# Encoder trunk on one core: output and down projections in 1024-column groups, seven block products for eight in 32 tile pairs

## The chip, the core and the metric

The kernel runs on one core of one Trainium2 chip. A core has a matrix engine (TensorE, PE in the profile), a vector engine (VectorE, DVE), an engine for activations and copies (ScalarE, ACT), a general engine (GpSimd, POOL) and an engine that here only issues DMAs (SyncE, SP). Each runs its own queue in order; they wait for one another through semaphores. Operands lie in SBUF; matmuls write to eight PSUM banks of 128 x 512 float32. The metric is the device time of one execution in microseconds (us), the median of several runs.

## The reference, cut to what matters

```
def mixer_block(x, ...):
    h = rms_norm(x, g_norm)
    uv, qkv, gates = split(h @ w_in)                 # 2048 -> 2048 | 3072 | 4096
    y_a = gmlp_branch(uv, ...)                       # u * (W_s LN(v) + b), 128-position chunks
    y_b = neighbourhood_attn(q, k, v, rpb)           # 16 heads, 4 x 16 window
    merged = sigmoid(g_a) * (y_a @ Wb_a) + sigmoid(g_b) * (y_b @ Wb_b)
    return x + merged @ w_out                        # "out": 2048 x 2048

def conv_ffn(x, ...):
    h = rms_norm(x, g_norm)
    up = conv3(h @ w_up)                             # "up": 2048 x 11008, depthwise over positions
    gate, val = split(up)
    return x + (silu(gate) * val) @ w_down           # "down": 5504 x 2048

out = rms_norm(conv_ffn(mixer_block(x, ...), ...), norm_final)
```

There is one layer, 256 positions (two blocks of 128), width 2048, all in float32.

## The kernel before, in words

Every product of float32 matrices is made of three matmuls. An operand is split into a high half, its rounding to the matmul's input type, and a low half, the rest: x = xh + xl, w = wh + wl. The products xh wh, xl wh and xh wl are summed in PSUM.

The weights are packed on the host into pieces of up to 128 x 1024 float32 (512 KB), in the order of use. For each piece SP issues a load into `wraw` (five buffers), ACT writes the high half `whi` as a copy, and DVE writes the low half `wlo` as wraw - whi. `begin(i)`, called ahead of the matmuls of piece i, issues the loads up to piece i + 5 and the splits up to piece i + 3, and runs the small tasks that were set for piece i with `at(i, f)`. So the order of all engines' work is that of one written program, whose unit is the piece. Buffers are reused in rotation.

There are two kinds of groups. In "nat" groups the activations are the stationary operand: for 512 output columns and both position blocks, two banks collect all rows of the weight; a piece is two weight tiles of 128 x 512 and takes 12 matmuls of 128 x 512. In "ws" groups the weights are stationary and the activations stream; these are u, q, k and the up-projection. The up-projection has 22 groups of two channel tiles (gate and value; the last has one), eight pieces each. After each, ACT and DVE add the banks' two halves, multiply by the norm, do the convolution (`conv`, lines 754 to 761), the gate (766, 767), and split the activation `a` (362, 363). Only after all 22 do the four down groups of 512 columns run over the 43 activation tiles. At a group's end `ev_down` adds the banks to x2 (line 781), squares the sum for the norm (782) and multiplies by the final gain (791). The output projection is the same with 16 tiles of `m`, and `ev_out` adds x (`xr`). The last group ends with its last four pieces in order of the position block, and `finish` scales and stores each block.

## Time and profile before

| | |
|---|---|
| runs | 1331.11 us median of 3 (1330.84 to 1331.73) |
| profiled execution | 1331.94 us, of which the instructions span 1329.9 |
| granted TensorE clock | 0.997 |
| DMA | 261.40 MB, mean 197 GB/s |
| stages in the span, us | start and value, u: 0 to 125; attention, gates, branches: 125 to 575; output: about 575 to 617; up: 617 to 1086; down: 1086 to 1321 |

In the page, the first part gives busy time per engine, the second the span in 40 slices (digits are tenths). The chain of waits is followed back from the last instruction. In a list of groups the columns are line, engine, operation, output <- inputs, shapes, count, busy us, mean ns of one, and the idle time ahead of them with what ended it. In the timeline the columns are start, length, engine, line. Matmuls overlap, so that their mean length is longer than the time from one to the next.

### The profile page before, as it was taken

To read this page: it belongs to the slowest core of one execution; us is meant where nothing else is said; L and a number is where in the kernel's file an instruction comes from. 1 tells how busy PE (TensorE), PEld (TensorE's weight loads), DVE (VectorE), ACT (ScalarE), POOL (GpSimd) and SP (SyncE) were. 2 spreads that over 40 slices of the span, in tenths; PEclk is the share of its full clock that TensorE was granted. 3 is DMA by queue.
4 is the path that set the end of the run, shared out by engine and by line. 5 is a ranking of instruction groups with operands and counts; after the bars stand their busy time and mean duration, and the time that the engine had idled before them with its cause. 6 is when DMAs were issued, how large, how long until landed. Compare 5 with 4: busy or idle time off the path is not lost.

```text
span 1329.9 us, 18442 instructions
## 1 busy us (share of the span) xinstructions
PE 1317.1 (99%) x6817; PEld 1124.5 (85%) x6817; DVE 868.5 (65%) x1248; ACT 721.8 (54%) x1059; POOL 100.2 (8%) x192
## 2 busy tenths in 40 slices
PE   8999999999999999999999999999999999999997
PEld 6888888888888888888888888888888888888885
DVE  6576667777564545555878787878787875545454
ACT  6755567576444444545656565656565564434342
POOL 0501065430000000000000000000000000000000
PEclk9999999999999999999999999999999999999998
DMA  9856786655666667666666666666666567656662
GB/s 359 280 185 183 212 225 180 202 159 180 187 189 189 193 189 224 206 201 181 188 190 189 191 189 190 189 191 188 191 186 193 164 196 222 211 186 205 190 199 95
DMA packets 77082, 261.40 MB, mean 197 GB/s; under 512 B 9792, under 2 KB 13760, under 8 KB 76736
## 3 DMA queue, kind: packets, MB, share of 16 engines
q1 hardware_dynamic: 72592, 252.40, 61.5%
q0 software_dynamic: 3968, 7.30, 2.4%
q8 instruction: 53, 0.87, 0.3%
q10 hardware_dynamic: 432, 0.53, 0.1%
q14 instruction: 37, 0.30, 0.1%
HBM read 256.00 MB, written 2.10 MB: 194 GB/s over the span
## 4 chain that ended last, share of the span: by engine, by line
PE 98%; DMA 1%; DVE 0%; SPq 0%; ACT 0%; issue 0%; DVEq 0%
PE bank L235 30%; PE bank L256 17%; PE bank L258 17%; PE bank L257 17%; PE bank L239 16%; DMA wraw<-in_weights_dram 1%; PE bank L592 1%; PE bank L642 0%; PE bank L468 0%; PE bank L730 0%; PE bank L688 0%; PE bank L632 0%; SPq L300 0%; DVE x L820 0%; SPq L177 0%; DVE wlo L192 0%
## 5 line engine op out<-in xcount | busy, mean ns | idle before, releaser
L192 DVE TENSOR_TENSOR wlo<-wraw,whi 128x1024 fp32r<-128x1024 f32 (+1 forms) x473 | 571.4, 1212 | 385.1 <-ACT whi L191 371.5
L191 ACT ACTIVATE whi<-wraw 128x1024 fp32r<-128x1024 f32 (+1 forms) x473 | 492.5, 1045 | 395.4 <-PE bank L257 278.2
L235 PE MATMUL bank<-h,whi 128*128 128x512 f32 x1760 | 423.1, 391 | 0.0
L235 PEld LDWEIGHTS bank<-h,whi 128*128 128x128 f32 x1760 | 322.9, 188 | 61.7
L239 PEld LDWEIGHTS bank<-h,wlo 128*128 128x128 f32 x1760 | 226.4, 191 | 9.0
L239 PE MATMUL bank<-h,wlo 128*128 128x256 f32 x1760 | 230.8, 283 | 0.0
L256 PE MATMUL bank<-whi,h 128*128 128x512 f32 x384 | 151.7, 395 | 0.9 <-ACT h L352 0.6
L257 PE MATMUL bank<-whi,h 128*128 128x512 f32 x384 | 150.0, 391 | 0.8 <-DVE h L359 0.8
L258 PE MATMUL bank<-wlo,h 128*128 128x512 f32 x384 | 150.0, 391 | 0.6 <-DVE wlo L192 0.5
L256 PE MATMUL bank<-whi,a 128*128 128x512 f32 x344 | 133.9, 389 | 0.0
L257 PE MATMUL bank<-whi,a 128*128 128x512 f32 x344 | 133.9, 389 | 0.0
L258 PE MATMUL bank<-wlo,a 128*128 128x512 f32 x344 | 133.9, 389 | 0.0
L256 PEld LDWEIGHTS bank<-whi,h 128*128 128x128 f32 x384 | 72.3, 188 | 16.4 <-ACT h L352 1.0
L257 PEld LDWEIGHTS bank<-whi,h 128*128 128x128 f32 x384 | 72.2, 188 | 16.4 <-DVE h L359 2.0
L258 PEld LDWEIGHTS bank<-wlo,h 128*128 128x128 f32 x384 | 72.1, 188 | 16.4 <-DVE wlo L192 1.5
L756 ACT ACTIVATE tc<-ta,vec 128x256 f32<-128x256 f32 x86 | 47.1, 595 | 70.1 <-DVE ta L754 70.1
L257 PEld LDWEIGHTS bank<-whi,a 128*128 128x128 f32 x344 | 64.6, 188 | 13.5
L256 PEld LDWEIGHTS bank<-whi,a 128*128 128x128 f32 x344 | 64.6, 188 | 13.3
L258 PEld LDWEIGHTS bank<-wlo,a 128*128 128x128 f32 x344 | 64.6, 188 | 13.3
L746 ACT ACTIVATE tb<-bank 128x256 f32<-128x256 f32 x86 | 28.3, 384 | 43.0 <-PE bank L235 42.7
L759 DVE SCALAR_TENSOR_TENSOR tc<-ta,vec,tc 128x255 f32<-128x255 f32 x86 | 41.4, 481 | 14.4 <-ACT tc L756 14.4
L959 POOL DMA_DIRECT2D gfin<-in_norm_final_dram x4 | 2.2, 549 | 642.9 <-DVE tc L767 535.5
(141 smaller groups left out, 1093.6 us busy)
## 6 DMA issues: line engine op xcount, KB each, us to landing
wraw<-in_weights_dram SPq DMA_DIRECT2D x459, 512.0 KB, 4.2
wraw<-in_weights_dram SPq DMA_DIRECT2D x14, 256.0 KB, 3.0
xs<-in_x_dram SPq DMA_DIRECT2D x2, 1024.0 KB, 9.0
vw<-va POOLq DMA_DIRECT2D x32, 64.0 KB, 6.2
xr<-in_x_dram POOLq DMA_DIRECT2D x4, 512.0 KB, 5.5
run<-in_rpb_dram POOLq DMA_DIRECT2D x64, 31.2 KB, 3.9
xk<-in_x_turned_dram SPq DMA_DIRECT2D x7, 256.0 KB, 7.8
gfin<-in_norm_final_dram POOLq DMA_DIRECT2D x4, 256.0 KB, 4.9
```

The source lines that it names most:

```text
L191: nc.scalar.activation(h[:, k, :m], w[:, k, :m], AF.Copy)
L192: nc.vector.tensor_sub(l[:, k, :m], w[:, k, :m], h[:, k, :m].bitcast(F32))
L235: nc.tensor.matmul(p, h[:, k - k0, b * 128:(b + 1) * 128], acts(k), start=k == 0, stop=k == nk - 1)
L239: nc.tensor.matmul(p[:, :T], l[:, k - k0, b * 128:(b + 1) * 128], acts(k)[:, 0, :], start=False, stop=False)
L256: nc.tensor.matmul(p, xh, h[:, kk, :m], start=st, stop=False)
L257: nc.tensor.matmul(p, xl, h[:, kk, :m], start=False, stop=False)
L258: nc.tensor.matmul(p, xh, l[:, kk, :m], start=False, stop=sp)
L592: nc.tensor.matmul(o, Q[s][:, c], k.rearrange("p (r c) -> p r c", r=ROWS)[:, :, k0:k0 + UNION], start=n == 0, stop=n == 1)
L746: nc.scalar.activation(t, p[:, T:], AF.Copy)
L756: nc.scalar.activation(v, u, AF.Identity, scale=ck[:, 1, ch:ch + 1], bias=ck[:, 3, ch:ch + 1])
L759: nc.vector.scalar_tensor_tensor(v[:, 1:], u[:, :T - 1], ck[:, 0, ch:ch + 1], v[:, 1:], op0=OP.mult, op1=OP.add)
L959: nc.gpsimd.dma_start(fin["g", j], bass.AP(tensor=norm_final.tensor, offset=norm_final.offset + j * 512, ap=[[0, 128], [1, 512]]))
```

## The change

**Groups of 1024 columns.** The value columns, the output and the down projection use "wide" groups: a piece is one weight tile of 128 x 1024, and four banks (two position blocks by two column halves) collect the sums. An ordinary piece takes 12 matmuls as before.

**Seven products.** A pair of tiles (256 rows of the weight) by two position blocks and two column halves is a 2 x 2 by 2 x 2 block product, eight block products of three matmuls. In four of the pairs of each wide group of output and down (`OUT_SEVEN`, `FF_SEVEN`; 8 pairs in the output, 24 in down) it is made of seven, of sums of blocks. The sums of activation blocks are made by GpSimd (`token_sums`) and split once; the sums of weight blocks are made by DVE from the two raw tiles, in place, for every pair and column group (`sums`): a half unit `half_hi`, `half_lo` (512 columns) and three units of 1024 (b, t, s) instead of two. The seven products go to eight banks, four of which collect parts that `combine` joins after the last such pair; the joined block `comb` is added to x2, by DVE or by a DMA that adds.

**Low halves by DMA.** Of the ordinary pieces in these groups every second (25 in all) gets its low half in another way: ACT writes -w rounded to `wlo`, a DMA of GpSimd's queue adds w to it.

**Three channel blocks.** Up and down alternate: 7 up groups and their part of down, 7 and theirs, 8 and theirs; down's sums are added to x2 after each block (six wide groups instead of four). 

**Queues.** Pieces are prepared up to i + 4, as far as units (four, six from the output on) are free; a raw buffer is loaded again as soon as the program has split it. Banks are handed out in the order in which they were freed. x is loaded into x2 by two DMAs, the four loads of `xr` are gone. At the start one chunk of x goes with each piece, instead of two.

```diff
+AHEAD = 5
+RAW, UNITS, HALVES = (5, 0), (4, 2), 2
+FF_BLOCKS = ((0, 14), (14, 28), (28, 43))
+FF_SEVEN = (0, 1, 3, 5)
+FF_ORDER = (0, 1, 2, 3, 4, 5, 6)
+OUT_SEVEN = (4, 5, 6, 7)
+OUT_ORDER = ((0, 1, 4, 5, 2, 6, 7, 3), (4, 5, 0, 6, 1, 7, 2, 3))
+LAST = 3
...
+            if i in by_dma:
+                nc.scalar.activation(l[:, :size], w[:, :size], AF.Copy, scale=-1.0)
+                nc.gpsimd.dma_start(l[:, :size], w[:, :size], accum_op=OP.add)
+                high(h[:, :size], w[:, :size])
+                raw_done(i)
+                return
...
+        def one():
+            slot = half_free.pop(0)
+            h, l = (slot[0].tile([128, 512], F32R, name=f"half_{p}{slot[1]}") for p in ("hi", "lo"))
+            halves[i] = (h, l, slot)
+            r0 = raw[i][0]
+            high(h, r0[:, c0])
+            low(l, r0[:, c0], h)
+            nc.vector.tensor_add(r0[:, c0], r0[:, c0], r0[:, c1])
+        def two():
+            r0, r1 = raw[i][0], raw[i + 1][0]
+            hb, lb = unit((i, "b"))
+            ht, lt = unit((i, "t"))
+            high(hb, r1)
+            nc.vector.tensor_add(r0[:, c1], r0[:, c1], r1[:, c1])
+            high(ht, r0)
+            low(lb, r1, hb)
+            nc.vector.tensor_add(r1[:, c1], r1[:, c1], r0[:, c0])
+            nc.vector.tensor_add(r1[:, c0], r1[:, c0], r1[:, c1])
+            low(lt, r0, ht)
+            raw_done(i)
+        def three():
+            r1 = raw[i + 1][0]
+            h, l = unit((i, "s"))
+            high(h, r1)
+        def four():
+            r1 = raw[i + 1][0]
+            h, l, _ = units[i, "s"]
+            low(l, r1, h)
+            raw_done(i + 1)
...
+        def combine():
+            c = fx["p"].tile([128, 4, 512], F32, name="comb")
+            nc.scalar.activation(c[:, 0, :], p(1), AF.Copy)
+            nc.vector.tensor_sub(c[:, 1, :], c[:, 0, :], p(6))
+            nc.vector.tensor_sub(c[:, 2, :], c[:, 1, :], p(7))
+            nc.vector.tensor_sub(c[:, 3, :], p(5), c[:, 2, :])
+            nc.vector.tensor_sub(c[:, 1, :], p(5), c[:, 1, :])
+            free(p(1), p(6), p(7), p(5))
...
+            if n in firsts:
+                product(1, acts(k, 0), (h, l))
+                product(5, S[0], (ht[:, c0], lt[:, c0]))
+                product(7, S[2], (ht[:, c1], lt[:, c1]))
...
+            elif n - 1 in firsts:
+                product(6, S[1], (hs[:, c1], ls[:, c1]))
+                product(2, acts(k + 1, 0), (hb[:, c0], lb[:, c0]))
+                product(3, S[3], (hb[:, c1], lb[:, c1]))
+                product(4, acts(k + 1, 1), (hs[:, c0], ls[:, c0]))
...
+    def token_sums(f, a11, a21, a12, a22):
+        nc.gpsimd.tensor_sub(f[:, 4, :], f[:, a21, :], f[:, a11, :])
+        nc.gpsimd.tensor_sub(f[:, 5, :], f[:, a21, :], f[:, a22, :])
+        nc.gpsimd.tensor_sub(f[:, 6, :], f[:, a11, :], f[:, 5, :])
+        nc.gpsimd.tensor_sub(f[:, 7, :], f[:, a12, :], f[:, 6, :])
...
+    def rest_by_dma(j):
+        def go(c):
+            nc.gpsimd.dma_start(rs["x2"][:, :, j * 1024:(j + 1) * 1024], c.rearrange("p (b a) t -> p b (a t)", b=2),
+                                accum_op=OP.add)
...
+    for j in range(2):
+        steps["out", j] = wide_step(("out", j), of_tiles(lambda k: mg["mT"][k]), lambda k: four_sums(fx["s", k], 0),
+                                    ("before", (rest_by_dma, rest_by_sums)[j](j)), ev_out(j))
...
+            rest = ("before", rest_by_sums(j)) if end else ("after", rest_by_dma(j))
+            steps["down", n, j] = wide_step(("down", n, j), down_acts, down_sums, rest, ev_down(n, j),
+                                            LAST if end and j == 1 else 0)
```

How the queues stand at the places of which the prediction speaks (a row is line, operation, output <- inputs, columns, and in brackets the engines and DMA queues that it waits for):

VectorE in the down projection before, at the change from one group of 512 columns to the next: low halves, the two additions into x2, two multiplies by the final gain.

```order
L192 TENSOR_TENSOR wlo<-wraw,whi 128x1024 [waits DMAHW1_49,PE_49,Activation_49]
L192 TENSOR_TENSOR wlo<-wraw,whi 128x1024 [waits DMAHW2_49,PE_49,Activation_49]
L781 TENSOR_TENSOR x_4942<-bank,x_4942 128x512 [waits PE_49] x2
L791 TENSOR_TENSOR x_4942<-x_4942,gfin 128x512 [waits DMASW4_49,Activation_49]
L791 TENSOR_TENSOR x_4942<-x_4942,gfin 128x512 [waits Activation_49]
L192 TENSOR_TENSOR wlo<-wraw,whi 128x1024 [waits DMAHW3_49,Activation_49]
```

VectorE now, at the change of column group in the first channel block: "one" of the next group's second pair (L245 into `half_lo`, L289), the last low half of its first pair, "two" of the second pair (L296 to the L245 ahead of L969), then the additions into x2 that empty the four banks.

```order
L245 TENSOR_TENSOR half_lo_7644<-wraw_7572,half_hi_7643 128x512 [waits DMAHW1_49,Activation_49]
L289 TENSOR_TENSOR wraw_7572<-wraw_7572 128x512 [waits DVE_49]
L245 TENSOR_TENSOR wlo_7641<-wraw_7550,whi_7640 128x1024 [waits PE_49]
L296 TENSOR_TENSOR wraw_7572<-wraw_7572,wraw_7574 128x512 [waits DMAHW2_49,DVE_49]
L245 TENSOR_TENSOR wlo_7664<-wraw_7574,whi_7663 128x1024 [waits PE_49,Activation_49]
L299 TENSOR_TENSOR wraw_7574<-wraw_7574,wraw_7572 128x512 [waits DVE_49]
L300 TENSOR_TENSOR wraw_7574<-wraw_7574 128x512 [waits DVE_49]
L245 TENSOR_TENSOR wlo_7666<-wraw_7572,whi_7665 128x1024 [waits PE_49,Activation_49]
L969 TENSOR_TENSOR x_4941<-bank_7390,x_4941 128x512 [waits PE_49]
L969 TENSOR_TENSOR x_4941<-bank_7394,x_4941 128x512 [waits PE_49]
L969 TENSOR_TENSOR x_4941<-bank_7398,x_4941 128x512 [waits PE_49]
L969 TENSOR_TENSOR x_4941<-bank_7483,x_4941 128x512 [waits PE_49]
```

A pair's two low halves have become eight instructions, and the additions stand behind a whole pair's preparation.

PE before, in a down group: a piece waits for its high half and its low half.

```order
L256 MATMUL bank_10499<-whi_10753,a32_5613 128x512 [waits Activation_49]
L257 MATMUL bank_10499<-whi_10753,a32_5613 128x512
L258 MATMUL bank_10499<-wlo_10754,a32_5613 128x512 [waits DVE_49]
L256 MATMUL bank_10499<-whi_10753,a33_5614 128x512
L257 MATMUL bank_10499<-whi_10753,a33_5614 128x512
L258 MATMUL bank_10499<-wlo_10754,a33_5614 128x512
```

PE now, at the place of the VectorE rows: the second half of the next group's first pair, products 6, 2, 3 and 4; banks 7717, 7721 and 7725 are those that the additions into x2 empty.

```order
L384 MATMUL bank_7713<-whi_7640,a_6146 128x512 [waits DVE_49,Activation_49]
L385 MATMUL bank_7713<-whi_7640,a_6146 128x512
L386 MATMUL bank_7713<-wlo_7641,a_6146 128x512 [waits DVE_49]
L384 MATMUL bank_7717<-whi_7609,a_6146 128x512 [waits DVE_49]
L385 MATMUL bank_7717<-whi_7609,a_6146 128x512
L386 MATMUL bank_7717<-wlo_7610,a_6146 128x512
L384 MATMUL bank_7721<-whi_7609,a_6146 128x512 [waits DVE_49]
L385 MATMUL bank_7721<-whi_7609,a_6146 128x512
L386 MATMUL bank_7721<-wlo_7610,a_6146 128x512
L384 MATMUL bank_7725<-whi_7640,a_6146 128x512 [waits DVE_49]
```

Three products now wait for DVE's additions, where before a group found its banks free.

More of the change, by code (lines that the diff above doesn't have):

```diff
@@ L962, in trunk_kernel @@
     fin["load"] = load_fin
[L963 to L967 removed]
+    at(starts["down", end, 1], sqrt_ready)
+    for i, piece in enumerate(pieces):
+        key = piece[0]
+        if i == starts[key] and key in before:
+            before[key]()
+        begin(i)
+        steps[key](i)
     finish_tasks()
```

725 lines of the change are left out of this document (454 added, 271 removed).

## The prediction

> **What bounds the kernel now.** First the page: busy shares, the slices, the chain of waits.
>
> ```profile
> PE 1317.1 (99%) x6817; PEld 1124.5 (85%) x6817; DVE 868.5 (65%) x1248; ACT 721.8 (54%) x1059; POOL 100.2 (8%) x192
> PE   8999999999999999999999999999999999999997
> DVE  6576667777564545555878787878787875545454
> PE 98%; DMA 1%; DVE 0%; SPq 0%; ACT 0%; issue 0%; DVEq 0%
> ```
>
> TensorE (PE) is the bound everywhere: 98% of the chain, no gaps but at both ends. VectorE (DVE) is next, and unevenly: 7 and 8 tenths in the up-projection (slices 20 to 32), 4 and 5 in the down-projection. The windows of the up stage and of one down group give numbers, and the timeline gives the rate of PE.
>
> ```profile
> 617.00:1077.00 460.00, 460.00 (x2645) 406.64 (x2644) 352.40 (x574) 268.65 (x413) 0.00 (x0) 1.00 0.62 185
> 1145.00:1203.00 58.00, 58.00 (x257) 48.04 (x257) 28.92 (x26) 23.70 (x26) 0.54 (x1) 1.00 0.61 199
> ...
> 1086.80 0.39 PE L256 MATMUL bank<-whi,a 128*128 128x512 f32 x1
> 1320.50 0.39 PE L258 MATMUL bank<-wlo,a 128*128 128x512 f32 x1
> ...
> L256 PE MATMUL bank<-whi,a 128*128 128x512 f32 x344 | 133.9, 389 | 0.0
> ```
>
> The columns after the length are busy us of PE, weight load, DVE, ACT, POOL. DVE is busy 77% of the up stage and 50% of a down group. The mean of 389 ns is not what a matmul costs, since they overlap: L256, L257 and L258 have 344 each, so 1032 start between 1086.80 and 1320.50, one per 233.7/1031 = 0.2267 us. This is the price that I use.
>
> The price of DVE is also read from start to start.
>
> ```profile
> 790.41 0.76 DVE L754 TENSOR_TENSOR ta<-ta,rb 128x256 f32<-128x256 f32 x2
> 791.50 0.49 DVE L759 SCALAR_TENSOR_TENSOR tc<-ta,vec,tc 128x255 f32<-128x255 f32 x1 [0.33 <-ACT tc L756]
> 792.02 0.48 DVE L761 SCALAR_TENSOR_TENSOR tc<-ta,vec,tc 128x255 f32<-128x255 f32 x1
> 792.43 0.48 DVE L759 SCALAR_TENSOR_TENSOR tc<-ta,vec,tc 128x255 f32<-128x255 f32 x1
> 792.94 0.48 DVE L761 SCALAR_TENSOR_TENSOR tc<-ta,vec,tc 128x255 f32<-128x255 f32 x1
> 793.34 1.22 DVE L192 TENSOR_TENSOR wlo<-wraw,whi 128x1024 fp32r<-128x1024 f32 x1
> 794.48 0.42 DVE L767 TENSOR_TENSOR tc<-tc 128x256 f32<-128x256 f32 x1
> 794.84 1.23 DVE L192 TENSOR_TENSOR wlo<-wraw,whi 128x1024 fp32r<-128x1024 f32 x1
> ...
> 808.37 1.42 DVE L748 TENSOR_TENSOR ta<-bank,tb 128x256 f32<-128x256 f32 x4 [1.17 <-ACT tb L746]
> ...
> 1081.16 0.69 DVE L192 TENSOR_TENSOR wlo<-wraw,whi 128x512 fp32r<-128x512 f32 x1
> 1081.76 0.42 DVE L767 TENSOR_TENSOR tc<-tc 128x256 f32<-128x256 f32 x1
> ```
>
> A low half of 1024 columns takes 1.14 us (793.34 to 794.48), one of 512 takes 0.60, a multiply of 256 takes 0.36. An instruction that waits for the one ahead of it starts 0.52 after it, one that doesn't 0.41: such a wait costs 0.11. A convolution step takes 2.93 (790.41 to 793.34).
>
> **The change, part by part.** PE: 32 pairs do 21 matmuls for 24, so 96 fall away: 96 x 0.2267 = **-21.8 us**. A seven-product pair takes 4.76 us of PE, a plain pair 5.44; an up piece stays (22.3 us for a full group of eight, half for the last).
>
> DVE, for a seven-product pair: three lows of 1024, one of 512, four sums of 512 (no row of before; nearest the 512 low): 3 x 1.14 + 5 x 0.60 = 6.4, and four waits on the instruction ahead: **6.9 us**, where the two lows of before were 2.3. Of this "one" is 1.4, "two" 4.3, the last low 1.1. A plain pair costs 1.14, its second piece being made by DMA. The change of DVE per pair is +4.6 while PE's share falls: a pair needs 2.1 us more of DVE than PE takes for it. A column group has 4 x 6.9 + 3 x 1.14 + 2.7 (four instructions that join the sums) + 2.45 (four additions into x2) = 36.2 us of DVE against 4 x 4.76 + 3 x 5.44 = 35.4 of PE. So in a down block DVE has no slack, and it enters with a debt, the convolutions of the last two up groups, against a lead of four or five pieces.
>
> *Blocks one and two.* Zero is when PE starts the last up group; PE would need the last low of the second column group at 22.3 + 70.7 - 5.4 - 2.7 = 84.9. DVE has until then 8 x 6.9 + 6 x 1.14 + 4.6 (four up lows) + 10.3 and 8.7 (evacuating two up groups: four additions 1.4 and in the first 1.2 of waiting, two convolutions, gates, splits) + 2.7 + 2.45 = 90.8. **5.9 us** can't be hidden by any order. Followed in the order that stands (adding the prices row by row, and each instruction waiting for its own): the first pair is ready in time; the second's low at 31.2 where PE wants it at 29.6, having waited 0.5 already; the third pair's first half at 40.3 for 39.4, its last low at 45.6 for 42.4; the fourth in time. That is 0.5 + 1.7 + 0.9 + 3.2 = 6.3. Then the change of group: the first product that needs a new bank comes 2.7 us into the pair, at 66.7, but the addition that empties the bank stands behind "two" of the next pair but one on DVE and ends at 70.6: +3.9. After it the second group is ahead. **+10.2 each**, 20.4.
>
> *Block three.* The last up group has half the columns: 11.1 us of PE while DVE must still do the convolutions of the group ahead. First pair ready at 17.5 for 11.1 (+6.4), then +1.2, +1.6, +1.3, +0.8, +0.6. At the change of group DVE also adds the joined sums to x2 (2 x 1.14), and each addition is now followed by its multiply, which waits for a square on ACT:
>
> ```profile
> 1146.13 1.28 DVE L781 TENSOR_TENSOR x<-bank,x 128x512 f32<-128x512 f32 x2
> 1147.39 0.19 ACT L782 ACTIVATION_READ_ACCUMULATOR junk<-x 128x1 f32 x1
> 1147.61 1.45 DVE L791 TENSOR_TENSOR x<-x,gfin 128x512 f32<-128x512 f32 x2 [0.19 <-ACT junk L782]
> ```
>
> From the first addition to the first multiply are 1.48 us, so each bank follows the last by 2.05. The third bank is free at 74.6 where PE could use it at about 65: 9.4, and 3 more for the next pair's low behind it. **+24.2**. The sum of DVE alone: 8 x 6.9 + 7 x 1.14 + 12.2 (the full group ahead, with four half-size lows) + 4.3 (the last group) + 5.0 (joining, and into x2) + 8 x 0.6 (additions and multiplies) = 89.5 against 11.1 + 76.2 - 10.9 = 76.4 of PE, 13.1 at least.
>
> *Output projection.* DVE: 8 x 6.9 + 5 x 1.14 + 2.4 (the last branch) + 2.6 (m and its sums split) + 2.7 + 2.45 + 3.4 (splitting the transposed x2) = 74.5 for 70.9 of PE, 3.6 at least. At the change of group the joined sums go to x2 by a DMA of 1 MB with addition, and the additions, and the transposes that PE has ahead of its next product, wait for it.
>
> ```profile
> xs<-in_x_dram SPq DMA_DIRECT2D x2, 1024.0 KB, 9.0
> xr<-in_x_dram POOLq DMA_DIRECT2D x4, 512.0 KB, 5.5
> ```
>
> Joined at 43.3, landed at 43.3 + 1 (issue) + 9.0 (the same size, without addition), three additions: 55.2, where PE stands at 45.0. With 2 us later for the transposes and the squares on ACT: **+12.3**, between 3.6 and 21 (twice the landing). The Trainium skill, "DMA: Bandwidth & Descriptors", section "Anatomy of one DMA", gives 2 us and bytes at 436 GB/s for this queue, by which 1 MB would be an estimated 4.4 us; the trace has 9.0 beside weight loads, and by the page's figure this term would be 7.7.
>
> *The 25 low halves made by DMA.*
>
> ```profile
> L191 ACT ACTIVATE whi<-wraw 128x1024 fp32r<-128x1024 f32 x459 | 483.9, 1058 | 383.5 <-PE bank L257 271.5 <-PE bank L235 92.7 <-DMA wraw<-in_weights_dram 7.5
> ```
>
> ACT gets a second copy of 1.06 for each; with 3.8 for a seven-product pair it does 4 x 3.8 + 9 x 1.06 = 25 us in a group of 35, so it stays clear. The 512 KB need 5.5 to, reading two sources, 9 us; the plain piece after two seven-product pairs has its buffer 7.5 us ahead and ACT's copy first, so 0 to 3 us late, in 8 places. Lateness there gives DVE time it lacks next: I take 0, and 20 as the other end.
>
> *The end.* The last two blocks of the output finish 2.05 us apart instead of 4.8 (nine matmuls for 21):
>
> ```profile
> 1320.92 0.69 DVE L781 TENSOR_TENSOR x<-bank,x 128x512 f32<-128x512 f32 x1 [0.43 <-PE bank L258]
> 1324.71 0.54 DVE L820 TENSOR_SCALAR x<-h,r,e 128x512 f32<-128x512 f32 x1
> ```
>
> One finish occupies DVE 4.3 us, so the second starts 2.4 to 3 us later: **+2.9**.
>
> *The start.* One x chunk per piece instead of two: 640 KB for 768.
>
> ```profile
> 0.00:45.00 45.00, 41.25 (x173) 32.61 (x174) 26.04 (x34) 30.27 (x51) 0.71 (x6) 1.00 0.96 371
> ```
>
> PE idles 3.75 us there, and the data that it waits for falls by a sixth: -0.7, between -2 and +1. The value columns in one group: same matmuls, 0. x goes to x2 directly, two DMAs on POOL's queue for four; twelve activation pairs split 896 columns for 512, 0.4 us on ACT and DVE in the up stage's slack: 0.
>
> *GpSimd's sums* (four of 128x128 for 16 pairs) lie under up pieces. What they do to DVE shows where POOL masks the bias:
>
> ```profile
> 194.56 0.50 POOL L557 TENSOR_SCALAR_AFFINE_SELECT bias<-bias 64x256 f32<-64x256 f32 x1
> 203.95 1.32 DVE L192 TENSOR_TENSOR wlo<-wraw,whi 128x1024 fp32r<-128x1024 f32 x1
> 204.28 1.36 POOL L557 TENSOR_SCALAR_AFFINE_SELECT bias<-bias 64x256 f32<-64x256 f32 x1
> ```
>
> The same select takes 1.36 for 0.50 beside a low, and the low 1.32 for 1.22: 0.1 per low, four lows a pair, hidden by DVE's 23% but for the last pairs before each block, 0.4 there: 0. The Trainium skill, "SBUF — State Buffer", section "Who interferes with whom", states that a VectorE instruction with two SBUF inputs and a GpSimd instruction that reads SBUF exclude each other for a whole instruction. The trace agrees on POOL's side; by the rule DVE could lose up to four POOL instructions of 0.5 us in each of the three last groups, an estimated 6 us more.
>
> Sum: -21.8 + 20.4 + 24.2 + 12.3 + 2.9 - 0.7 = **+37.3**. The profiled execution took 1331.94 (span 1329.9), 0.8 over the median of 1331.11; +37.3 on the median is 1368.4.
>
> **Rivals.**
> *A: only DVE's sum counts, order costs nothing.* 2 x 5.9 + 13.1 + 3.6 = 28.5 instead of 56.9: 1340. For it: six units of buffer, and a PE that waits lets DVE get ahead. Against: additions behind "two" in a queue that runs in order.
> *B: faster.* It needs cheaper pairs. Per 0.1 us on a pair the four stages change by 8 x 0.1 each, 3.2 in all; with order's costs as they are the balance is at 5.7 us a pair, under A at 6.6. For it: my sums of 512 have no row; at 0.35 us (what four of 256 from PSUM take each, 1.42/4) the four cost 1.0 less, 5.9, and with A's order no stall is left, 1331.1 - 21.8 + 2.2 = 1311.5; with half of that cheapness 1324. Against: the 512 low has the same two SBUF inputs and takes 0.60.
> *C: the DMA sums bind.* If 512 KB with addition lands in 12 us, the eight early places lose 3 or more and the 1 MB lands 9 later: +20 and +9, 1388 to 1397. Against: the xr row.
>
> **How the numbers follow.** The order as followed 0.62, A 0.16, B 0.12, C 0.10. Two per mille (2.7 us) is what can be told from no change. The forecast is 1368, its own range 1352 to 1383; with A and C 1334 to 1393, which leaves out B and the far end of C. Faster 0.12, same 0.03 (the edge between A and B), slower 0.85.
>
> **What would show it.** Right: in the down blocks of the changed kernel DVE busy at nine tenths and more, PE at eight to nine; PE waiting for low halves from DVE; at each change of column group one wait of 4 us (blocks one, two), about 9 (block three) and about 10 (output) for additions to x2; seven-product pair at 6.9 us of DVE. B is right if the sums of 512 start 0.4 us apart; C if PE's waits name the DMA queue of the low halves. The forecast is wrong if DVE shows idle time in the down blocks while PE runs without gaps.

## The result, and the profile after

The changed kernel takes 1425.58 us (median of four, 1424.38 to 1426.46) against 1331.28 for the kernel before: ratio 1.0708, interval 1.0689 to 1.0726. It is slower, as forecast, but by 94 us, not 37; the time lies outside the range that was given (1334 to 1393).

First the page of the changed kernel: busy shares, the slices of PE, DVE and the granted clock, the chain, the two costliest groups that wait, and the transfers that are new.

```profile
PE 1337.3 (94%) x6721; PEld 1125.6 (79%) x6721; DVE 1024.6 (72%) x1450; ACT 790.1 (55%) x1141; POOL 187.4 (13%) x284
PE   9999999999999998699999888999988899998875
DVE  5586667766645569677878886687889668788777
PEclk9999999999999999799999899999998999999978
PE 72%; DVE 9%; issue 7%; DMA 6%; ACT 5%; SPq 0%; POOL 0%; DVEq 0%; ACTq 0%; POOLq 0%
...
L386 PE MATMUL bank<-wlo,a 128*128 128x512 f32 x296 | 126.0, 426 | 26.9 <-DMA wlo<-wraw 14.9
L384 PE MATMUL bank<-whi,a 128*128 128x512 f32 x296 | 125.8, 425 | 22.8 <-DVE x L969 12.6
...
wlo<-wraw POOLq DMA_DIRECT2D x25, 512.0 KB, 7.7
x<-comb POOLq DMA_DIRECT2D x5, 1024.0 KB, 12.1
```

PE's share of the chain falls from 98% to 72%, and the gaps stand in four places only: slices 16 and 17 (output) and the three down blocks. PE is busy 20 us longer than before though it has 96 matmuls fewer; the mean of a down matmul rises from 389 ns to between 418 and 426, and PEclk shows 7 and 8 where it had shown 9. VectorE (DVE) is at 8 and 9 tenths in the first two slices of blocks one and two, but at 6 in the third (slices 25 and 32), where PE has gaps as well: DVE's work alone doesn't explain them.

The timeline of PE in block one shows what a wait looks like and what follows it (the number in brackets is the idle time ahead, and what ended it).

```profile
788.25 0.39 PE L384 MATMUL bank<-half_hi,a 128*128 128x512 f32 x1
...
790.74 0.39 PE L386 MATMUL bank<-wlo,a 128*128 128x512 f32 x1
794.54 0.80 PE L384 MATMUL bank<-whi,a 128*128 128x512 f32 x1 [3.41 <-DVE ta L685]
795.13 0.63 PE L385 MATMUL bank<-whi,a 128*128 128x512 f32 x1
795.55 0.63 PE L386 MATMUL bank<-wlo,a 128*128 128x512 f32 x1
...
800.67 0.45 PE L386 MATMUL bank<-wlo,a 128*128 128x512 f32 x1
800.96 0.39 PE L384 MATMUL bank<-whi,a 128*128 128x512 f32 x1
...
815.05 0.79 PE L386 MATMUL bank<-wlo,a 128*128 128x512 f32 x1 [2.58 <-DVE wlo L245]
...
841.99 0.80 PE L384 MATMUL bank<-whi,a 128*128 128x512 f32 x1 [3.12 <-DVE x L969]
...
858.49 0.56 PE L386 MATMUL bank<-wlo,a 128*128 128x512 f32 x1 [4.77 <-DMA wlo<-wraw]
...
883.78 1.98 PE L369 MATMUL bank<-h,whi 128*128 128x512 f32 x8
```

There are four kinds of wait: for a bank that DVE empties after the last up group (L685), for a low half made by DVE, for a bank of the group ahead (the additions, L969), and for a low half made by DMA. After the longer ones matmuls start 0.427 us apart (795.13 to 795.55), for 0.227: thirteen of them here, 133 in the whole program, each some 0.2 us later than at full pace. My first reading was: 133 x 0.2 = 26.6 us for the clock, the rest for idling.

A stage is measured from the start of its first product to that of the next stage (block one: 788.25 to 883.78, 95.5), block three to the end of its last product. TensorE's own work in it is 70.8 in blocks one and two, 76.4 in block three and 84.3 in the output: the lengths of the kernel without pairs (e1 below) less 8 x 0.68. In us:

| kernel | output | block 1 | block 2 | block 3 | whole |
|---|---|---|---|---|---|
| TensorE's work with 32 pairs | 84.3 | 70.8 | 70.8 | 76.4 | |
| changed kernel | 112.2 | 95.5 | 95.3 | 108.8 | 1425.6 |
| e1 no pairs | 89.7 | 76.2 | 76.2 | 81.8 | 1334.4 |
| e2 waits filled | 111.5 | 95.3 | 94.9 | 109.4 | 1424.9 |
| e4 plain pair first | 117.4 | 90.9 | 92.1 | 101.5 | 1414.1 |
| e5 lows by DVE | 113.7 | 89.9 | 89.9 | 107.3 | 1413.0 |
| e6 no DMA | 112.4 | 88.0 | 89.0 | 104.5 | 1405.3 |
| e7 sixth raw buffer | 113.0 | 94.3 | 95.8 | 107.2 | 1421.8 |
| e9 highs swapped | 108.5 | 93.7 | 94.0 | 106.9 | 1416.8 |
| e10 output sums by DVE | 111.5 | 94.5 | 96.0 | 111.3 | 1426.1 |
| e11 no weight sums | 107.7 | 81.3 | 82.8 | 93.9 | 1380.9 |
| e12 four mended | 109.1 | 84.2 | 84.8 | 97.6 | 1388.9 |
| e13 output order | 101.7 | 95.1 | 96.4 | 110.5 | 1415.5 |
| e14 five mended | 97.7 | 84.2 | 85.0 | 97.2 | 1380.4 |
| e15 eight pairs | 89.7 | 73.4 | 73.4 | 81.8 | 1329.1 |
| e16 fourteen pairs | 87.0 | 73.4 | 73.4 | 80.8 | 1325.3 |

So the loss over TensorE's work is 27.9, 24.7, 24.5 and 32.4, 109.5 in all, where the prediction had 12.3, 10.2, 10.2 and 24.2.

### The profile page after: what moved, and what is told of

The parts are those of the page before. It is cut to its first block, busy times and chain, and to the rows that moved or that the text cites. A ratio compares the mean times of both kernels' runs of the same rounds, so it can differ in the third digit from the quotient of the medians.

```text
span 1424.7 us, 18744 instructions
## 1 busy us (share of the span) xinstructions
PE 1337.3 (94%) x6721; PEld 1125.6 (79%) x6721; DVE 1024.6 (72%) x1450; ACT 790.1 (55%) x1141; POOL 187.4 (13%) x284
## 4 chain that ended last, share of the span: by engine, by line
PE 72%; DVE 9%; issue 7%; DMA 6%; ACT 5%; SPq 0%; POOL 0%; DVEq 0%; ACTq 0%; POOLq 0%
PE bank L369 26%; PE bank L375 13%; PE bank L386 10%; PE bank L384 10%; PE bank L385 10%; DVE wlo L245 4%; DMA wlo<-wraw 4%; ACT whi L242 2%; DMA wraw<-in_weights_dram 2%; DVE half_lo L245 1%; DVE wraw L299 1%; DMA x<-comb 1%; PE bank L819 0%; DVE x L969 0%; ACT tc L1025 0%
## 5 line engine op out<-in xcount | busy, mean ns | idle before, releaser
L245 DVE TENSOR_TENSOR wlo<-wraw,whi 128x1024 fp32r<-128x1024 f32 (+1 forms) x478 | 577.4, 1221 | 239.7 <-ACT whi L242 231.7
L242 ACT ACTIVATE whi<-wraw 128x1024 fp32r<-128x1024 f32 (+1 forms) x503 | 518.0, 1045 | 300.6 <-PE bank L385 124.4
L386 PE MATMUL bank<-wlo,a 128*128 128x512 f32 x296 | 126.0, 426 | 26.9 <-DMA wlo<-wraw 14.9
L386 PE MATMUL bank<-wlo,h 128*128 128x512 f32 x384 | 150.6, 392 | 0.5 <-DVE wlo L245 0.5
L384 PE MATMUL bank<-whi,a 128*128 128x512 f32 x296 | 125.8, 425 | 22.8 <-DVE x L969 12.6
L385 PE MATMUL bank<-whi,a 128*128 128x512 f32 x296 | 123.7, 418 | 0.0
L386 PEld LDWEIGHTS bank<-wlo,a 128*128 128x128 f32 x296 | 60.9, 206 | 47.3 <-DMA wlo<-wraw 18.7
L384 PEld LDWEIGHTS bank<-whi,a 128*128 128x128 f32 x296 | 60.7, 205 | 39.9 <-DVE x L969 15.2
L936 POOL TENSOR_TENSOR full<-full 128x128 f32<-128x128 f32 x16 | 17.2, 1076 | 528.2 <-DVE full L1037 349.3
L386 PEld LDWEIGHTS bank<-wlo,h 128*128 128x128 f32 x384 | 72.4, 189 | 16.6 <-DVE wlo L245 1.4
L683 ACT ACTIVATE tb<-bank 128x256 f32<-128x256 f32 x110 | 36.1, 383 | 73.2 <-PE bank L369 67.7
L685 DVE TENSOR_TENSOR ta<-bank,tb 128x256 f32<-128x256 f32 x110 | 39.1, 417 | 45.8 <-ACT tb L683 45.6
L385 PEld LDWEIGHTS bank<-whi,a 128*128 128x128 f32 x296 | 61.0, 206 | 13.0
## 6 DMA issues: line engine op xcount, KB each, us to landing
x<-comb POOLq DMA_DIRECT2D x5, 1024.0 KB, 12.1
x<-in_x_dram POOLq DMA_DIRECT2D x2, 1024.0 KB, 12.6
```

Of the source, the lines that this page charges most:

```text
L242: nc.scalar.activation(h, w, AF.Copy)
L245: nc.vector.tensor_sub(l, w, h.bitcast(F32))
L384: nc.tensor.matmul(p, xh, wh, start=start, stop=False)
L385: nc.tensor.matmul(p, xl, wh, start=False, stop=False)
L386: nc.tensor.matmul(p, xh, wl, start=False, stop=stop)
L683: nc.scalar.activation(t, p[:, T:], AF.Copy)
```

## The experiments

**e1: the regrouping without the pairs.**

```diff
-FF_SEVEN = (0, 1, 3, 5)
+FF_SEVEN = ()
-OUT_SEVEN = (4, 5, 6, 7)
+OUT_SEVEN = ()
...
-            by_dma.update(...)
+            pass
```

> The changed kernel without any seven-product pair and without low halves by DMA: 1024-column groups, three channel blocks, the new start and end are left, each weight piece is split as before and each output block gets its three products, so the result is computed in full. By the prediction's own terms this is the end (+2.9) and the start (-0.7), no shortage of DVE: 1332 to 1335, and the 94 us belong to the pairs and their joining. Rival: the blocks themselves cost, since each down block now starts with banks and convolutions of the up group that has just ended (the 3.41 and 3.15 us waits for L685, doubled by the slower matmuls behind them): then 1340 to 1350, with these two waits still in the trace.

1334.43, 3.1 over before (ratio 1.0023, 1.0013 to 1.0032). Groups of 1024 columns and three blocks cost nothing but the end, which takes 12.0 us after the last product for 9.0. So the pairs, with the low halves made by DMA, cost 91 us, although they take 21.8 from TensorE.

**e2: useless products fill the waits.**

```diff
+    def fill(p, n, start=False):
+        for _ in range(n):
...
+            nc.tensor.matmul(p, zero["z"], v.rearrange("p a t -> p (a t)"), start=start, stop=start)
...
         nc.tensor.matmul(p, xl, wh, start=False, stop=False)
+        fill(p, n)
         nc.tensor.matmul(p, xh, wl, start=False, stop=stop)
```

A table gives n, 4 to 20, at 22 places (ahead of a product's first matmul or, as here, ahead of its last); 35 more stand ahead of the output's transposes.

> The changed kernel with useless products of TensorE (a zero weight, added to an open bank, nothing changes in the sum) put directly ahead of the 22 matmuls that waited 1 us or more and ahead of the transposes that waited 8.45, so many that they take about the wait (0.2267 us each). Theory, idle time lowers the clock: the 133 matmuls that started 0.427 us apart behind such waits go back to 0.227, which is worth up to 133 x 0.2 = 26.6 us where nothing else is late; 1399 to 1412. Rival, VectorE sets the pace and the slow matmuls cost nothing: the matmuls run at 0.227 but the next waits grow by as much, 1420 to 1428. Other rival, the slowness comes from something else than idling: 0.427 stays in the trace and the time is 1424 or more.

1424.93. From the page and the timeline of this kernel:

```profile
PE 1372.5 (96%) x6970; PEld 1153.8 (81%) x6970; DVE 1025.7 (72%) x1450; ACT 790.1 (56%) x1141; POOL 187.7 (13%) x285
PEclk9999999999999999999999999999999999999998
```
```profile
804.69 0.63 PE L418 MATMUL bank<-wlo,a 128*128 128x512 f32 x1 [2.06 <-DMA wlo<-wraw]
...
830.65 0.50 PE L418 MATMUL bank<-wlo,a 128*128 128x512 f32 x1 [1.33 <-DMA wlo<-wraw]
...
855.95 0.50 PE L418 MATMUL bank<-wlo,a 128*128 128x512 f32 x1 [1.42 <-DMA wlo<-wraw]
```

The clock is back at 9 everywhere, and every stage is as long as it was, within 0.7 us: the matmuls are fast again and then wait for halves at new places (804.69, 830.65) or, behind their fillers, longer at an old one (855.95). So idling is what lowers the clock, since filling the idle time brings it back, and the slow matmuls cost nothing here. My first reading fell: whatever comes late sets the pace, and TensorE has time.

**e3: what a gap costs where TensorE is the bound.** The kernel before, with this at twelve places in its down-projection:

```diff
+        nc.tensor.transpose(p[:, :128], z[:, :128], ident)
+        for _ in range(n):      # 3, 6, 9, 12, 15, 18
+            nc.gpsimd.memset(z, 0.0)
+        nc.tensor.transpose(p[:, 128:256], z[:, :128], ident)
```

(`z` stands for a small tile of zeros, shortened here.)

> The kernel before with twelve gaps made in TensorE's work in its down-projection, where nothing else is late: a transpose, 3, 6, 9, 12, 15 or 18 fillings of a small tile by GpSimd that wait for it (0.3 us each, so gaps of about 1 to 6 us, two of each length), and a transpose that waits for them. Theory: a gap under about 1.5 us costs its own length, one over 2.5 costs its length and then 6 to 13 matmuls at 0.427 for 0.227, 1.2 to 2.6 us more: twelve gaps of 3.3 us on average make 40, eight of them with about 2 us more 16, two transposes each 2 to 5 in all: 1385 to 1395. Rival: a gap costs only its length, 1370 to 1378, with all matmuls 0.227 apart.

1402.86, 71.5 over before, more than expected, since the gaps were longer (4.0 us on average). The second transpose in the timeline, with its wait:

```profile
1104.03 0.33 PE L298 MATMUL bank<-ident,zz 128*128 128x128 f32 x1 [1.24 <-POOL zz L297]
...
1117.73 0.33 PE L298 MATMUL bank<-ident,zz 128*128 128x128 f32 x1 [2.33 <-POOL zz L297]
...
1205.54 0.48 PE L298 MATMUL bank<-ident,zz 128*128 128x128 f32 x1 [6.77 <-POOL zz L297]
```

The twelve waits (six lengths from 1.24 to 6.77, twice) sum to 48.0 us, and the stage grew by 71.9 (306.0 for 234.1). Counting starts more than 0.3 us apart behind each wait gives no slow run after 1.24 us, and 6 to 11 slow matmuls after any of 2.33 or more, about 19 us in all. So here the clock does cost, 2 us a gap. The same thing has a price in one kernel and none in the other.

**e4: a plain pair first in each column group.**

```diff
-FF_ORDER = (0, 1, 2, 3, 4, 5, 6)
+FF_ORDER = (2, 0, 1, 4, 3, 5, 6)
-OUT_ORDER = (..., (4, 5, 0, 6, 1, 7, 2, 3))
+OUT_ORDER = (..., (0, 4, 5, 6, 1, 7, 2, 3))
```

> The changed kernel with only the tables of the order altered: each column group of a down block, and the second group of the output, begins with a plain pair, which needs four banks at first and not seven (FF_ORDER 2,0,1,4,3,5,6). Theory: the waits of 3.41, 3.15, 3.12, 4.14 and 4.42+0.43+0.49 us at the second product of the second piece are for banks that DVE frees behind the sums of the next pairs; with a plain pair first they go, 19.2 us and the slow matmuls behind them (37 to 45 x 0.2 = 8): 1398 to 1405. Rival: DVE has only this much time, so what isn't waited for at a bank is waited for at a low half of the pair after it: 1418 to 1428.

1414.14, between the two. The waits for banks are gone, and the blocks are 4.6, 3.2 and 7.3 us shorter; low halves take over part of the wait (2.91, 0.87, 1.72 us in block one). The output grew by 5.2: its wait at the change of group is 11.20 us there for 8.45. Why one plain pair makes it longer, no run shows.

**e5, e6, e7: the DMA-made halves and the raw buffers.**

```diff
 e5:  by_dma stays empty
 e6: -    nc.gpsimd.dma_start(l[:, :size], w[:, :size], accum_op=OP.add)
 e7: -RAW, UNITS, HALVES = (5, 0), (4, 2), 2
     +RAW, UNITS, HALVES = (5, 1), (4, 2), 2     # the sixth from the up-projection on
```

> The changed kernel with all low halves made by VectorE (by_dma left empty, nothing else). After the filled waits cost nothing, the question is what sets the pace of 95.4 us in blocks one and two (70.7 of TensorE). Theory, the raw buffer: a low half made by DMA keeps its raw buffer until the DMA has landed, and SP's queue, which goes in order, waits for that 169.3 us in 25 times, with all later weight loads behind it; without these DMAs a buffer is free after a split, and VectorE's sum is the limit: a column group 36.2 + 3 x 1.14 = 39.6 us, a block about 89, 1395 to 1412. Rival, VectorE's sum and its order alone set the pace: 25 x 1.14 = 28 us more, 1440 to 1455.

> The changed kernel without the 25 DMAs of the low halves: the scalar engine's two copies stay, and the low half stays the negated copy, so that part of the result is left out; VectorE does exactly what it did. Theory, the raw buffer: the buffer is free after the copies and loads run ahead; blocks one and two from 95.4 to 78 to 86 us, block three from 108.8 to 92 to 100, output 112.2 to 104 to 109: 1370 to 1390. Rival, VectorE's sum and order: only the waits that name the DMA go (16.4 us in all, some of it taken up by the next low half), 1412 to 1424.

> The changed kernel with a sixth raw weight buffer from the first up-projection group on (the last norm's scale columns go to the room of the normed activations, which nobody needs by then, to make space). Theory, the raw buffer: a load is issued one piece (2.4 us) earlier, and a held buffer delays less: the three blocks 4 to 8 us shorter each, output unchanged, 1402 to 1414. Rival, VectorE: 1423 to 1428.

1413.04 (1 us above its range), 1405.32 and 1421.81. What had led to them is this chain in the changed kernel, from SP's waits over the whole program, and from the timelines of ACT and DVE in block one:

```profile
SPq L225 <- DMA wlo<-wraw: 169.3, 25, 12.5
```
```profile
864.38 0.63 ACT L242 ACTIVATE half_hi<-wraw 128x512 fp32r<-128x512 f32 x1 [6.55 <-DMA wraw<-in_weights_dram]
```
```profile
865.05 0.69 DVE L245 TENSOR_TENSOR half_lo<-wraw,half_hi 128x512 fp32r<-128x512 f32 x1 [8.30 <-ACT half_hi L242]
```

A raw buffer stays held until the DMA has landed, SP's queue waits for it in order, the next weights come late, and VectorE, which is short of time, stands still for 8.3 us. VectorE's waits for the high half of a late weight (`half_lo` for `half_hi`) are 10.8 us in block one of the changed kernel, 4.2 in e6 and none in e5.

The transfer that held the buffer here was itself late, and GpSimd's queue shows behind what:

```profile
844.29 1.18 POOL L955 DMA_DIRECT2D x<-comb  x1 [18.73 <-issue]
846.32 0.90 POOL L255 DMA_DIRECT2D wlo<-wraw  x1 [0.85 <-ACT wlo L254]
```

The 1 MB of joined sums landed at 855.97, the 512 KB of the low half at 858.45, 12.1 us after their issue, and SP issued the next load at 858.50. Block two has the same (12.6 us). The other 23 of these DMAs landed after 4.5 to 9.5 us. So in the second column group the low half for the first plain pair queues behind the joined sums of the first group; no run with the DMA-made halves takes this 1 MB out of the down blocks.

By e6 the 25 DMAs cost 20.3 us; VectorE makes the same halves for 28.5 us (25 x 1.14) of its own work and the kernel is still 12.5 faster. But the sixth buffer brought 3.8, not the 11 to 24 expected, and e6 stayed above its range. So the held buffer is only a part; how the 20 us divide between the held buffer and the lateness of the half itself is open.

**e8: two pairs in each down group, none in the output, no DMA lows** (FF_SEVEN = (3, 5)).

> The changed kernel with seven-product pairs at two of the seven places of each down group, in its middle (FF_SEVEN 3 and 5), none in the output, and all low halves by VectorE. TensorE has 12 x 0.68 = 8.2 us less than in the kernel without pairs (1334.4). VectorE needs 2 x 6.9 + 10 x 1.14 + 2.7 + 2.45 = 30.4 us of 36.7 in a group, so theory: nothing waits, 1326 to 1329, faster than before. Rival: the raw buffers that a pair holds (its second piece until the last low half) make loads late even without DMA lows, 1332 to 1345.

1336.54, 2.1 over e1: the rival's time, but its mechanism is not seen. Blocks one and two are 1.4 shorter than in e1, not 2.7, with one wait of 0.72 for a low half in each; block three is 2.6 longer. With the order of e9 the same eight pairs have no wait of PE left (e15, 73.4 us a block), though ScalarE's waits for loads in block one are much the same (4.0 us for 5.7).

**e9: the high half of a pair's last sum after the next piece's own.**

```diff
-            if late: queue.append((i, 1, 0, late[0]))
             queue.append((i, 1, 0, split_piece(i)))
-            if late: queue.append((i, 0, 0, late[1]))
+            if late: queue.append((i, 1, 0, late[0])); queue.append((i, 0, 0, late[1]))
```

(The same ahead of a pair's first step.)

> The changed kernel with one thing altered in the order: the high half of a pair's last sum is made after the next piece's own high half, not ahead of it. As it stands VectorE's next low half waits about 1.0 us after each pair, since ScalarE waits for VectorE's last sum first (8.0 us in 9 waits of wlo for whi in block one, 3 more at half_lo for half_hi). Theory, VectorE's path with these round trips sets the pace: 6 to 8 us off each of the four stages, 1396 to 1405. Rival, the DMA-made halves and the loads behind them set it: the round trips are covered, 1420 to 1427.

1416.76, 8.8 less, a third of what was expected. DVE's waits in block one, of the changed kernel and of e9 (us in total, times, longest):

```profile
DVE half_lo L245 <- ACT half_hi L242: 10.8, 3, 8.3
DVE wlo L245 <- ACT whi L242: 7.5, 8, 1.6
```
```profile
DVE half_lo L245 <- ACT half_hi L242: 13.5, 4, 9.4
DVE wlo L245 <- ACT whi L242: 3.8, 6, 1.2
```

Half of the wait of the round trips went (7.5 to 3.8), and the wait for late weights, 13.5 for 10.8, took most of it back in this block.

**e10: the output's joined sums added by VectorE.**

```diff
-("before", (rest_by_dma, rest_by_sums)[j](j))
+("before", rest_by_sums(j))
```

> The changed kernel with the joined sums of the first output group added to x2 by VectorE (two additions, 2.3 us) instead of the 1 MB DMA. Theory: the 12.1 us of the DMA stand ahead of the three additions, the transposes and the second group, so the output stage falls from 112.2 to 102 to 105 us, 1415 to 1418. Rival: the second group is late by VectorE's work in any case, 1421 to 1427.

1426.14: nothing. My theory of the output fell. The timeline of DVE in the changed kernel shows why:

```profile
567.91 0.68 DVE L459 TENSOR_TENSOR comb<-bank,comb 128x512 f32<-128x512 f32 x1
568.51 0.68 DVE L245 TENSOR_TENSOR half_lo<-wraw,half_hi 128x512 fp32r<-128x512 f32 x1
...
574.16 1.22 DVE L245 TENSOR_TENSOR wlo<-wraw,whi 128x1024 fp32r<-128x1024 f32 x1
578.66 2.48 DVE L969 TENSOR_TENSOR x<-bank,x 128x512 f32<-128x512 f32 x4 [3.28 <-DMA x<-comb]
```

Between the joined sums (568.5) and the four additions stand 6.8 us of weight work for the next group's pairs. The DMA adds 3.28 to that; VectorE's two additions add 2.3 instead.

**e11: without the four sums of weights** (L289, L296, L299, L300 taken out).

> The changed kernel without the four sums of weights in each pair; their places keep the unsummed weights, so the products of the pairs are left false, and everything else (three lows of 1024, one of 512, the highs, the DMA lows, the banks) stays. VectorE has 4 x 0.65 = 2.6 us less for each of 32 pairs, and ScalarE's highs wait for no sum. Theory, VectorE's path sets the pace: 8 x 2.6 = 21 and some 8 us of round trips less to do in each stage, so that the stages come down to what DMA lows and banks cost, 78 to 86 us for blocks one and two; 1355 to 1385. Rival, DMA lows and raw buffers set it: 1400 to 1420.

1380.94, as the theory had it: 44.6 us from VectorE's path alone (its sums, and ScalarE's waits for them), with DMA lows and bank order as they were.

**e12: e5, e9, e10 and the down blocks' part of e4 together.**

> The changed kernel with four alterations at once: all low halves by VectorE, the high half of the last sum after the next piece's, plain pairs first in the down blocks, the output's joined sums added by VectorE. All 32 seven-product pairs stay. Theory: what is left is VectorE's sum, by the prediction's prices 90.8 + 6 x 1.14 = 97.6 us from the last up group on against 84.9 of TensorE, 13 us in blocks one and two, about 20 in block three, 10 in the output: 1334 - 21.8 + 56 = 1369, range 1362 to 1382; slower than before still. Rival, the waits were the smaller part and the pair itself costs VectorE more than 6.9 us: 1385 to 1400.

1388.88, above the range and within the rival's. But the rival's reason, a dearer pair, is not it: the blocks came out as summed (84.2, 84.8 and 97.6; 13.4, 14.0 and 21.2 over TensorE's work, where 13, 13 and 20 were expected). The output stayed at 109.1, 24.8 over, where 10 were expected.

**e13, e14: the second output group in the order of the first**, so that two plain pairs are ahead of its first seven-product pair; e13 is e10 with that, e14 is e12 with that.

```diff
-OUT_ORDER = ((0, 1, 4, 5, 2, 6, 7, 3), (4, 5, 0, 6, 1, 7, 2, 3))
+OUT_ORDER = ((0, 1, 4, 5, 2, 6, 7, 3), (0, 1, 4, 5, 2, 6, 7, 3))
```

> The changed kernel with the output's joined sums added by VectorE and the second output group in the order of the first, two plain pairs ahead of its first seven-product pair. Theory: what held the output's change of group is the place of the four additions on VectorE, behind the weight work of the next group's two seven-product pairs (10 us), not the DMA alone; behind plain pieces they come early: the output stage 111.5 to 98 to 104 us, 1411 to 1418. Rival: VectorE's sum is the limit, and the wait comes back at low halves: 1421 to 1427.

> As e12_all_fixes, with the second output group in the order of the first too. The blocks stay at 84, 85 and 98 us, which is VectorE's sum; the output stage falls from 109.1 to 96 to 101 us if the place of the additions is its cause: 1376 to 1382. Rival, VectorE's sum is the limit there too: 1386 to 1390.

1415.54 and 1380.35. The output falls to 101.7 and 97.7, and PE's wait for the additions at its change of group, 7.49 us in e10, is gone in e13: their place was what held it. In e14 block one looks like this, in the windows (length, then busy PE, weight load, DVE, ACT, POOL) and in PE's waits:

```profile
775.70:860.00 84.30, 74.34 (x314) 57.69 (x313) 80.56 (x104) 46.30 (x56) 1.25 (x1) 1.00 0.59 185
```
```profile
PE bank L384 <- DVE wlo L245: 8.7, 11, 1.4
PE bank L382 <- ACT whi L242: 1.3, 1, 1.3
```

The changed kernel has in its block one:

```profile
788.20:883.80 95.60, 81.16 (x314) 64.61 (x314) 74.71 (x97) 51.02 (x61) 6.33 (x7) 0.89 0.68 192
```

VectorE is busy 80.6 of 84.3 us there, for 74.7 of 95.6, and PE waits in many small steps for its low halves. This is the bound that the prediction summed, alone at last, with 25 low halves more on VectorE.

**e15, e16: fewer pairs, where VectorE has slack.** e15 has the pairs at places 3 and 5 of blocks one and two only; e16 adds place 3 in block three and pairs 4 and 5 of each output group. Both have e5's and e9's changes, e16 also e10's.

```diff
-FF_SEVEN = (0, 1, 3, 5)
+FF_SEVEN = ((3, 5), (3, 5), (3,))        # by block; e15: ((3, 5), (3, 5), ())
-OUT_SEVEN = (4, 5, 6, 7)
+OUT_SEVEN = (4, 5)                        # e15: ()
-OUT_ORDER = ((0, 1, 4, 5, 2, 6, 7, 3), (4, 5, 0, 6, 1, 7, 2, 3))
+OUT_ORDER = ((0, 1, 4, 2, 5, 3, 6, 7), (0, 1, 4, 2, 5, 3, 6, 7))    # e16 alone
```

> Eight seven-product pairs alone: places 3 and 5 of each group of down blocks one and two, none in block three and in the output; all low halves by VectorE; the high half of the last sum after the next piece's. VectorE has slack in these groups (about 30 of 36.7 us), so nothing should wait: 8 x 0.68 = 5.4 us less than without pairs (1334.4), 1328 to 1331. Rival: each pair still costs a wait of about 0.7, 1332 to 1336.

> As e15_few, with one seven-product pair more in each group of block three (place 3) and two in each output group (pairs 4 and 5, two plain pairs ahead of them), and the output's joined sums added by VectorE: 14 pairs, 9.5 us less TensorE than without pairs: 1325 to 1328 if VectorE keeps up everywhere. Rival: the output, where VectorE also turns x2, and block three, which starts late, wait: 1330 to 1340.

1329.08 (ratio 0.9983, 0.9974 to 0.9992) and 1325.33 (0.9960, 0.9946 to 0.9974): both beat the kernel before, by 2.3 and 6.0 us; the first is less than the 2.7 us that the prediction had set as the least to be told from no change, though its interval leaves out 1. Page and windows of e16, the last up group and block one:

```profile
PE 1308.1 (99%) x6775; PEld 1116.2 (84%) x6775; DVE 965.8 (73%) x1367; ACT 735.7 (56%) x1076; POOL 130.1 (10%) x222
PE   9999999999999999999999999999999999999996
DVE  5587667767564547896878798687879868686976
```
```profile
738.00:760.20 22.20, 22.20 (x129) 19.63 (x128) 17.86 (x28) 12.61 (x20) 4.54 (x4) 1.00 0.53 172
760.20:833.60 73.40, 73.40 (x325) 60.82 (x324) 66.48 (x85) 41.22 (x49) 1.25 (x1) 1.00 0.65 210
```

VectorE is as busy as in the changed kernel (73% for 72%), but in no stage over TensorE: no gap of PE in the output or the blocks, with 66.5 of DVE beside 73.4 of PE in block one.

## Why the prediction was wrong

*Right, and measured.* That VectorE would have no slack, and that this would outweigh TensorE's gain. The gain: 0.67 us a pair in e15 ((1334.43 - 1329.08) / 8) and 0.65 in e16, 0.68 predicted. The end: +3.0 for +2.9 in e1 (in the changed kernel itself +4.8, from 9.0 to 13.8 us after the last product). The regrouping: nothing. A seven-product pair on DVE: 6.9 predicted; between these two rows lies one pair's work:

```profile
834.46 0.68 DVE L245 TENSOR_TENSOR half_lo<-wraw,half_hi 128x512 fp32r<-128x512 f32 x1
...
841.25 2.48 DVE L969 TENSOR_TENSOR x<-bank,x 128x512 f32<-128x512 f32 x4
```

That is 6.79 us. And VectorE's sum: what the prediction said that no order can hide is 28.5 us (2 x 5.9 + 13.1 + 3.6), and 25 low halves of 1.14 are 28.5 more. With the order mended and those halves on VectorE, e14 loses 13.4, 14.2, 20.8 and 13.4 over TensorE's work, 62 us, with VectorE busy 96% of a block. So the prices held. That the prediction's own losses also add up to 57 is luck: half of that stood for the order, with the 25 halves on the DMA. The changed kernel is 45 us slower than e14.

*Where the sum fell short.* Its three large terms, +20.4 (blocks one and two), +24.2 (block three) and +12.3 (output), measured 49.2, 32.4 and 27.9.

*Failed: the 25 low halves made by DMA, of which it says "I take 0".* Taken away they give 20.3 us (e6), replaced by VectorE 12.5 (e5). The median landing, 7.7 us, is within the bounds given (5.5 to 9), but two landed after 12.1 and 12.6, behind the joined sums in their queue, and PE's two longest waits for such a half, 4.77 and 4.48 us, are for these. The cover failed too: the piece no longer "has its buffer 7.5 us ahead" where ACT waits 6.55 for a load. The other end, 20, is near what e6 gives. The step also asked only who waits for the half, not what the transfer holds meanwhile: the raw buffer, and through SP's queue every load behind it. Rival C, with 10%, also counted only the lateness of the halves. Its sign was there (14.9 of the 26.9 us that PE waits at L386 are for this DMA), its condition, 12 us a landing, only twice, and the 1 MB of the output was not late.

*Failed: the output's +12.3, "the joined sums go to x2 by a DMA of 1 MB".* The loss was 27.9. The DMA of the output landed after 9.4 us, where 10.0 were taken (12.1 is the median of all five), and the waits around the change of group (8.45, 0.72, 1.55 and 1.99 us) are near the "about 10" named. So the size was right and the cause not: without the DMA nothing changed (e10), and with the additions ahead of the pairs 10 us went (e13). Another 7.3 us are waits for low halves within the first group, for which the term had nothing. The prediction had the rule itself, additions behind "two" in an order that is kept, and used it for the down blocks; in the output it stopped at the first cause found.

*Failed: the order as followed in the blocks.* That "the first pair is ready in time" looked at the low halves alone. What came late was a bank: a seven-product pair opens seven, four are free, and the other four are emptied by DVE (L685) behind the next pair's work, 3.41 and 3.15 us at the start of blocks one and two. And the waits within a pair were priced at 0.11 each, from convolution steps on one engine; a sum on DVE, its high half on ACT and the low half on DVE is a round trip in which DVE stands still for about 1.0 at the end of each pair (7.5 us in 8 waits). Reordering gave 11.4 (e4) and 8.8 (e9). The wait at the change of group was right in size (3.12 and 4.14 for 3.9), and in block three too high (5.3 for 9.4).

*The four mendings taken alone* give 12.5 + 11.4 + 8.8 + 10.6 (e13 against e10) = 43.3, or 48.5 without the 5.2 that e4 lost in the output; together, without that loss, they give 45.2 (e14).

*Not in the prediction: the clock.* It fell where the prediction had nothing on it, and it cost nothing (e2).

*The rivals.* A fell, since order costs: e4, e9 and e13 change little but the order and gain 11.4, 8.8 and 10.6 us. (Its 1340 was not run as such: e14, 40 us above it, also has the 25 low halves on VectorE.) B fell with the pair at 6.8. The marks named beforehand: DVE at nine tenths holds at the starts of the blocks only, and the idle time of DVE beside a PE with gaps, seen in the last thirds of blocks one and two, was the sign that a third thing was late.

## What to carry to other kernels

Trading TensorE's time for VectorE's pays pair by pair, as long as VectorE's sum for that stretch, with what it brings from the stretch ahead, stays under TensorE's: over the kernel without pairs fourteen gave 9.1 us, thirty-two took 91, and still 46 in the best order tried. Where both engines show gaps in the same stretch, look for what is late to both: a transfer that holds a buffer, an evacuation behind other work in a queue that keeps its order, a round trip between engines; and price each by undoing it alone, since a wait on the list (or a slowed matmul) may be nothing but cover for the next one. For an operation put on a DMA, ask what it holds until it lands.

## What the runs showed of the hardware

- In e3 TensorE's matmuls slowed down behind both gaps of 2.33 us (8 or 9 of them 0.427 us apart, then 0.227) and behind every longer one, and not behind the two of 1.24 us; a gap of 6.77 us costs little more (11). The length alone doesn't decide: in the changed kernel a gap of 2.76 us (at 542.69) was followed by no slow matmul, while all over 3 us in the output and the blocks were followed by some. The Trainium skill, "TensorE: Matmul & The Clock Gate", section "HAM oscillation — how this bites in real kernels", warns of gaps over about 3.4 us; here 2.33 could be enough. The same page of the Trainium skill, section "Wait — 56ns, not 53.3ns?", gives 426.7 ns for 512 columns at its slow rate, half of full; the 0.427 seen here agrees.
- Products with a zero weight keep the clock up as well as real ones (e2, PEclk 9 in all slices but the last, as before).
- 512 KB added by DMA from SBUF into SBUF landed after 4.5 to 12.6 us (median 7.7), 1 MB after 9.4 to 12.9 (median 12.1), beside weight loads. By the fit in "DMA: Bandwidth & Descriptors", section "Anatomy of one DMA", of the Trainium skill the two would be an estimated 3.2 and 4.4 us.
- GpSimd's sums of 128x128 took 1.08, 1.05, 1.19 and 0.60 us on average (0.45 at the least), where the estimate was 0.5 for each. Of the 35 low halves of 1024 columns that VectorE made beside them 22 took 1.22 us as elsewhere, 12 took 1.48 and one 1.34: 3.3 us in all, most of it in up groups, where VectorE has slack. Beside the last sums ahead of block one VectorE's instructions grew by 0.6 us. So the 6 us that the prediction worked out from the rule on SBUF's shared port (the Trainium skill, "SBUF — State Buffer", section "Who interferes with whom") are not seen; VectorE does lose, but less, and GpSimd more.
